# Mixer of a streaming conv encoder: branch a's output tiles ahead of its last six gate tiles, which become three block pairs

## The chip, the cores and the metric

The kernel runs on one core of one Trainium2 chip. The metric is the device time of one launch in microseconds (us). TensorE (PE in the profile) multiplies, VectorE (DVE) adds and multiplies elementwise, ScalarE (ACT) does activations, casts and scaled copies, GpSimd (POOL) here issues accumulating transfers and small copies, and SyncE (SP) issues the loads of the weights. Each engine works through its instructions in program order.

## The reference, cut to what matters

```python
x = x + 0.5 * swiglu_ffn(rms_norm(x, ffn1_norm), ...)          # first FFN
h = rms_norm(x, mix_norm);  p = h @ w_in                        # 1024 -> 7 * 1024
a_b, a_c, a_v, b_u, gate_a, gate_b = split(p)
y_a = (a_b * causal_depthwise_conv3(a_c * a_v)) @ w_a_out
glu = b_u[..., :D] * sigmoid(b_u[..., D:])
b_conv = causal_depthwise_conv31(glu)
b_act = silu(layer_norm(b_conv + bias, ln_g, ln_b))
y_b = b_act @ w_b_out
x = x + (sigmoid(gate_a) * y_a + sigmoid(gate_b) * y_b) @ w_out
x = x + 0.5 * swiglu_ffn(rms_norm(x, ffn2_norm), ...)           # second FFN, then a final norm
```

There are 512 prompt rows and 64 sample rows, T = 576 together; D is 1024 and everything is fp32.

## The kernel before

Features lie on the 128 partitions and the 576 rows of x along them, so a 1024-feature activation is eight tiles of 128x576 (KT = 8, KU = 4). A product of one output tile is a sum over the eight input tiles. To keep fp32 accuracy every operand is split into a high part (cast to fp32r, by ScalarE) and a low part (what the cast lost), and three matmuls (high x high, high x low, low x high) are made for each of two halves of 288 columns. A **plain tile** is therefore 8 x 3 x 2 = 48 matmuls of 128x288. For a pair of output tiles there is a second form, the **block pair**: a 2x2 block product with seven multiplications instead of eight (Winograd's form of Strassen's algorithm), where the two output tiles and the two column halves are the blocks. It takes seven blocks of 4 x 3 = 12 matmuls, each with weights of its own (four of the seven are sums of the loaded ones) and moving operands of its own (some are sums of the input's halves, made by `Forms`). VectorE combines the seven results q[0] to q[6] into the two tiles. The two FFNs are made of block pairs for the most part; in the mixer before the change only two pairs of branch b's output (`block_pair`) are.

**Weight units.** `Stream` takes the weights through in units of four k-chunks (128x512). A unit's load goes over SP's queue into one of six raw tiles. Then `begin` casts the high part (ScalarE), and for a unit planned with "dma" ScalarE writes the negative of the high part and GpSimd adds the raw weights onto it by an accumulating transfer; for a unit planned with "dve", `end` lets VectorE subtract. `add` makes the sums of a block pair (VectorE). `get(n)` comes just ahead of the matmuls of unit n and calls `lead`, which ends the units up to n+5, adds up to n+7 and begins up to n+6 (`ahead` is 6 here). The parts go to tiles "u" (pool of four, one per unit) or to two tiles of another pool ("act", 44 of 128x576). A raw tile is loaded anew when its last reader is through.

**Order of work.** The order is the program's, on each engine. `product` issues the matmuls of a tile, then runs the evacuation (`then`) of the product before it (`take`), then `fill` takes steps out of the list `work` as long as a planned VectorE clock lags the planned TensorE clock. PSUM has four tiles of two banks (`psum2`); a block takes one bank.

**The mixer.** Eight tile pairs of p3/p4 (branch b's value and gate), whose 31-tap convolution is in `work`, then for branch a the tiles of p1, p2, p0. In the stretch that the change is about the kernel does, for j = 0 to 7, `product(("p", 5, j))` (gate a; `ga_of` takes the sigmoid) and `product(("ya", j))` (`ya_of` multiplies by the gate into M[j], which is the tile of X[j]). Between them `advance()` carries the LayerNorm of branch b through its stages: gather the sum, multiply it by ones on TensorE (`total`), the mean `mu`, eight `center` steps (subtract, square on ScalarE, add), gather the squares, and `rstd` (again a product with ones, then a root on ScalarE and three VectorE steps) for RL. After that come eight gate b tiles `product(("p", 6, j))` with the steps of `swish` in `work`, then yb (plain, block, plain, block pair) and the product with w_out.

The two lines of the loop that set the order, and the plan's homes of gate b's units:

```python
product(("p", 5, j), xg, ga_of(j))
advance()
product(("ya", j), AB, ya_of(j))
advance()
few = cycle(("u", "u", "u", "act"))
```

Of the kernel before, what the change touches and what calls it, by code (L numbers as in the profile page):

```python
# [9 lines left out]
F32 = mybir.dt.float32  # L10
F32R = mybir.dt.float32r
I32 = mybir.dt.int32
AF = mybir.ActivationFunctionType
ALU = mybir.AluOpType

P = 128
D = 1024
KT = D // P
# [4 lines left out]
KU = KT // 2  # L23
T = SEQ + DSEQ
# [89 lines left out]
def tile_encoder_step(  # L114
# [7 lines left out]
    pe, dve, sca, pool = (  # L122
        Ordered(tc, e, c)
        for e, c in (
            (nc.tensor, pe_cost), (nc.vector, dve_cost), (nc.scalar, None), (nc.gpsimd, None)
        )
    )
# [13 lines left out]
    def nm(s):  # L141
        uid[0] += 1
        return f"{s}_{uid[0]}"
# [4 lines left out]
    def gtile(dt=F32, n=LB, at=0):  # L148
        return conv.tile([P, 640], dt, tag="g", name=nm("g"))[:, at : at + n]
# [10 lines left out]
    def wtile(dt=F32, n=LB - HB):  # L160
        return conv.tile([P, LB - HB], dt, tag="w", name=nm("w"), bufs=6)[:, :n]

    def ttile(dt=F32):
        return tmp.tile([P, T], dt, tag="tmp", name=nm("tmp"))
# [13 lines left out]
    def halves(ap):  # L178
        return ap.rearrange("p (s n) -> p s n", s=2)

    def half(ap, s):
        return ap[:, s * H : (s + 1) * H]
# [148 lines left out]
    def home(other):  # L331

        homes[0] += 1
        return ("u", other)[homes[0] % 2]
# [24 lines left out]
    def plan_block(name, raws, homes, lows=("dma", "dma", "dma")):  # L359

        a21, a22, a11, a12 = raws
        s1, s2, s3, s4 = ((name, n) for n in range(1, 5))
        plan[name] = [
            ws.unit(src, KU, home, how, sums)
            for home, (src, how, sums) in zip(homes, (
                (a11, lows[0], ((s1, (a21, a22)),)),
                (s2, "dve", ((s2, (s1, a11)),)),
                (s1, "dve", ()),
                (s3, "dve", ((s3, (a11, a21)),)),
                (a12, lows[1], ()),  # L370
                (s4, "dve", ((s4, (s2, a12)),)),
                (a22, lows[2], ()),
            ))
        ]
        for n, unit in enumerate(plan[name]):
            second = n in (1, 5, 6)
            ws.places[unit] = (SHIFT, 0) if second else (0, SHIFT)
# [26 lines left out]
    def plan_mixer(name, w, col, home_of=None, low="dma"):  # L404
        plan_tile(name, w, 0, (KU, KU), col, "act", home_of, low)
# [4 lines left out]
    for j in range(KT):  # L410
        for b in (1, 2, 0):
            plan_mixer(("p", b, j), w_in, b * D + j * P)
    for j in range(KT):
        plan_mixer(("p", 5, j), w_in, 5 * D + j * P)
        plan_mixer(("ya", j), w_a_out, j * P)

    few = cycle(("u", "u", "u", "act"))
    for j in range(KT):
        plan_mixer(("p", 6, j), w_in, 6 * D + j * P, few)


# [44 lines left out]
    def block(w, xs):  # L466

        q = bank()[:, :H]
        for k in range(KU):
            (whi, wlo), (xh, xl) = w, xs[k]  # L470
            for m, (l, r) in enumerate(((whi, xh), (whi, xl), (wlo, xh))):
                pe.matmul(q, l[:, k, :], r, start=k == m == 0, stop=k == KU - 1 and m == 2)
        return q
# [10 lines left out]
    def take():  # L484

        while behind:
            ready, then = behind.pop(0)
            dve.time = max(dve.time, ready)
            then()
# [11 lines left out]
    def product(name, xs, then=None, order=None, got=None, soon=None):  # L501


        if name in early:
            return early.pop(name)[:, :, :H]
        ps = psum2()
        if order:
            got = chunks(name)
            for n, k in enumerate(order):
                mm(ps, *got[k], xs[k], n == 0, n == len(xs) - 1)  # L510
        else:
            turn, turning[0] = turning[0], False
            k = 0
            for n in plan[name]:
                w = None
                if not got:
                    w = ws.get(n)
                end = k + ws.units[n][1]
                k0 = k
                while k < end:  # L520
                    w = got[k][0] if got else w
                    if turn and k == 0:
                        turned(ps, w, xs)
                        k += 2
                        continue
                    mm(ps, w, k - k0, xs[k], k == 0, k == len(xs) - 1)
                    k += 1
                    if soon and k == 1:
                        soon()
        take()  # L530
        if then is None:
            dve.time = max(dve.time, pe.time)
            return ps[:, :, :H]
        fill()
        behind.append((pe.time, lambda: then(ps[:, :, :H])))
# [15 lines left out]
    def high(v):  # L551
        hi = atile(F32R)
        sca.copy(hi, v)
        return hi

    def low(v, hi):
        lo = atile(F32R)
        dve.tensor_tensor(lo, v, hi.bitcast(F32), op=ALU.subtract)
        return lo
# [115 lines left out]
    class Forms:  # L675
# [21 lines left out]

        def split(self, p):
            self.parts[p] = [(hi, low(v, hi)) for v, hi in self.t.pop(p)]

        def operands(self, xg):

# [444 lines left out]
    def center(j, mu):  # L1147

        dve.tensor_tensor(C[j], C[j], mu, op=ALU.subtract)
        var.square(C[j])  # L1150
        var.add(dve)

    def swish(i, RL, sig={}):

        if i < KT:
            dve.tensor_tensor(C[i], C[i], RL, op=ALU.mult)
            sig[i] = ttile()
            sca.activation(sig[i], C[i], AF.Sigmoid, scale=par(i, R_LG), bias=par(i, R_LB))
        j = i - 1
        if 0 <= j < KT:  # L1160
            dve.tensor_scalar(
                C[j], C[j], par(j, R_LG), par(j, R_LB), op0=ALU.mult, op1=ALU.add
            )
            dve.tensor_tensor(sig[j], sig[j], C[j], op=ALU.mult)
            BA.append(high(sig[j]))
        j = i - 2
        if 0 <= j < KT:
            BA[j] = (BA[j], low(sig[j], BA[j]))
            forms.b.setdefault(j // 2, []).append(sig[j])

    def ga_of(j):
        def then(ps):
            t = gates[j] = ttile()
            sca.activation(halves(t), ps, AF.Sigmoid)
        return then

    def ya_of(j):
        def then(ps):
            dve.tensor_tensor(halves(M[j]), ps, halves(gates.pop(j)), op=ALU.mult)
        return then  # L1180

    stage, held = [0], [0]

    def advance():

        nonlocal var, mu, RL
        if stage[0] == 0 and len(C) == KT and not work:
            lnsum.gather()
        elif stage[0] == 1:
            mu = ttile()  # L1190
            sca.mul(halves(mu), lnsum.total(), 1.0 / D)
            turning[0] = True
            var = Sum()
            work.extend((lambda i=i: center(i, mu)) for i in range(KT))
        elif stage[0] == 2 and not work:
            var.gather()
        elif stage[0] == 3 and not held[0]:
            held[0] = 1
            return
        elif stage[0] == 3:  # L1200
            RL = rstd(var)
            turning[0] = True
        else:
            return
        stage[0] += 1

    var = mu = RL = None
    for j in range(KT):
        if j == 5:
            while len(C) < KT:  # L1210
                work.pop(0)()
        product(("p", 5, j), xg, ga_of(j))
        advance()
        product(("ya", j), AB, ya_of(j))
        advance()
    take()
    sca.dma_start(hist.rearrange("(j p) n -> p j n", p=P), hst)
    while stage[0] < 4:
        while work:
            work.pop(0)()  # L1220
        advance()
    for i in range(KT + 2):
        work.append(lambda i=i: swish(i, RL))

        if i in (3, 5):
            work.append(lambda p=(i - 3) // 2: forms.combine(p))
        if i in (4, 6):
            work.append(lambda p=(i - 4) // 2: forms.split(p))
    ws.ahead = 4

    def gb_of(j):
        def then(ps):
            while work and j >= 2 and len(BA) < j - 1:
                work.pop(0)()
            sg = wtile(n=T) if j < 2 else gtile(n=T)
            sca.activation(halves(sg), ps, AF.Sigmoid)
            SGB.append(sg)
        return then

    for j in range(KT):  # L1240
        product(("p", 6, j), xg, gb_of(j))
    while work:
        work.pop(0)()
    for p in range(KU // 2, KU):
        forms.combine(p)
    take()
    for p in range(KU // 2, KU):
        forms.split(p)
# [227 lines left out]
```

## Time and profile before

| | |
|---|---|
| median of 3 runs | 1287.54 us (1287.22 to 1287.66) |
| profiled execution, its own time | 1287.41 us |
| its span | 1285.6 us |
| busy: TensorE, VectorE, ScalarE, GpSimd | 1275.0, 927.8, 762.8, 357.2 us |
| matmuls | 9728 |
| mean granted TensorE clock | 0.998 |

The span is the time from the first to the last instruction of the profiled execution; 1.8 us of its own time lie outside. All positions in the text are microseconds from the start of that span. In the stretch in question gate a and ya run from about 643.4 to 744.4, gate b to 794.3, yb after it. In a row of the timeline the first number is the start, the second the length, then engine, line, operation, written tile <- read tiles, form and count; the bracket gives the idle time of the engine ahead of it and what ended that. All rows have line 90, since one helper issues every instruction.

### The profile page before, as it was taken

The page shows a single profiled execution, that of the slowest core. Times are in us where ns is not written, and L with a number is a line of the kernel's source. Part 1 is how long each engine was busy: PE and PEld are TensorE (multiplying, and loading weights), DVE is VectorE, ACT ScalarE, POOL GpSimd, SP SyncE. Part 2 cuts the span into 40 slices and gives each one's busy share as a digit, 9 for nine tenths or more (in the row PEclk, how much of TensorE's full clock was granted, in tenths as well). Part 3 has the DMA queues.
Part 4 walks back from the last instruction along what each step waited for, and adds up shares of the span by engine and source line. Part 5 has one row for each costly group of instructions (what it writes and reads, how often), then busy time and mean ns, then how long its engine had stood idle before and what let it go on. Part 6 is the DMA issues. An engine that isn't in the chain of part 4 may idle for free.

```text
span 1285.6 us, 25688 instructions
## 1 busy us (share of the span) xinstructions
PE 1275.0 (99%) x9728; PEld 1273.3 (99%) x9728; DVE 927.8 (72%) x1544; ACT 762.8 (59%) x1354; POOL 357.2 (28%) x455
## 2 busy tenths in 40 slices
PE   9999999999999999999999999999999999999997
PEld 9999999999999999999999999999999999999996
DVE  6868668748846998888895166756967848847955
ACT  7645646646776645555444576467665655654664
POOL 0032332332333444333321221122142141241230
PEclk9999999999999999999999999999999999999999
DMA  7287786886799898878885767686597696796693
GB/s 222 69 181 154 164 181 154 178 183 147 157 225 230 173 207 166 172 168 177 169 169 124 170 137 160 147 207 147 132 177 174 147 203 147 165 207 140 153 181 93
DMA packets 286091, 213.94 MB, mean 166 GB/s; under 512 B 15376, under 2 KB 248848, under 8 KB 285968
## 3 DMA queue, kind: packets, MB, share of 16 engines
q0 software_dynamic: 55440, 91.12, 43.3%
q1 hardware_dynamic: 228784, 120.35, 32.9%
q8 instruction: 77, 1.26, 0.4%
q10 hardware_dynamic: 1744, 0.83, 0.2%
q14 instruction: 46, 0.38, 0.1%
HBM read 116.17 MB, written 4.98 MB: 94 GB/s over the span
## 4 chain that ended last, share of the span: by engine, by line
PE 98%; DMA 1%; DVE 0%; ACT 0%; SPq 0%; DVEq 0%; issue 0%
PE mm L90 98%; DMA x<-in_x_dram 0%; DMA gains<-in_params_dram 0%; DVE g L90 0%; DVE tmp L90 0%; SPq L730 0%; DVE act L90 0%; ACT act L90 0%; DVEq L1466 0%; DVE r L90 0%; DVE x L90 0%; ACT tmp L90 0%; ACT r L90 0%
## 5 line engine op out<-in xcount | busy, mean ns | idle before, releaser
L90 PE MATMUL mm<-act,u 128*128 128x288 f32 x4758 | 666.2, 293 | 0.0
L90 PEld LDWEIGHTS mm<-act,u 128*128 128x128 f32 x4758 | 637.2, 188 | 0.0
L90 PE MATMUL mm<-act,g 128*128 128x288 f32 x3030 | 431.5, 293 | 0.0
L90 PEld LDWEIGHTS mm<-act,g 128*128 128x128 f32 x3030 | 408.9, 188 | 0.3 <-DMA g<-raw 0.2
L90 POOL DMA_DIRECT2D u<-raw x194 | 169.3, 873 | 477.1 <-ACT u L90 311.6
L90 PE MATMUL mm<-act,act 128*128 128x288 f32 (+2 forms) x1896 | 258.8, 293 | 0.5 <-DVE act L90 0.3
L90 PEld LDWEIGHTS mm<-act,act 128*128 128x128 f32 x1896 | 251.1, 188 | 1.1 <-DVE act L90 0.6
L90 ACT CAST u<-raw 128x512 fp32r<-128x512 f32 (+2 forms) x207 | 118.9, 575 | 172.3 <-PE mm L90 142.0
L90 POOL DMA_DIRECT2D g<-raw x124 | 107.8, 869 | 302.5 <-ACT g L90 246.4
L90 DVE SCALAR_TENSOR_TENSOR w<-g,prm,w 128x606 f32<-128x606 f32 x232 | 179.3, 842 | 1.4 <-ACT w L90 1.4
L90 DVE TENSOR_TENSOR tmp<-mm,tmp 128x288 f32<-128x288 f32 (+1 forms) x251 | 112.7, 457 | 67.3 <-PE mm L90 50.9
L90 ACT ACTIVATE u<-u 128x512 fp32r<-128x512 f32 (+2 forms) x194 | 115.0, 593 | 6.2
L90 ACT CAST g<-raw 128x512 fp32r<-128x512 f32 (+2 forms) x136 | 75.1, 552 | 45.6 <-DMA raw<-in_ffn_w_down_dram 16.3
L90 DVE SCALAR_TENSOR_TENSOR tmp<-mm,r 128x576 f32<-128x576 f32 x48 | 36.3, 756 | 74.8 <-PE mm L90 74.8
L90 POOL DMA_DIRECT2D act<-raw x67 | 59.1, 883 | 107.9 <-ACT act L90 94.2
L90 ACT CAST act<-tmp 128x576 fp32r<-128x576 f32 x92 | 61.9, 675 | 43.6 <-DVE tmp L90 42.5
L90 ACT CAST g<-w 128x512 fp32r<-128x512 f32 x79 | 49.0, 620 | 63.4 <-DVE w L90 55.8
L90 ACT CAST u<-w 128x512 fp32r<-128x512 f32 x81 | 50.2, 619 | 59.5 <-DVE w L90 43.3
L90 DVE TENSOR_TENSOR act<-tmp,act 128x576 fp32r<-128x576 f32 x92 | 67.5, 754 | 18.4 <-ACT act L90 16.8
L90 ACT ACTIVATE g<-g 128x512 fp32r<-128x512 f32 (+2 forms) x124 | 70.9, 572 | 3.9
L90 DVE TENSOR_TENSOR w<-raw,raw 128x512 f32<-128x512 f32 x82 | 56.1, 684 | 16.6 <-DMA raw<-in_ffn_w_gate_up_dram 12.1
L90 ACT ACTIVATE tmp<-tmp 128x576 f32<-128x576 f32 x47 | 32.2, 685 | 44.1 <-DVE tmp L90 44.1
(86 smaller groups left out, 833.4 us busy)
## 6 DMA issues: line engine op xcount, KB each, us to landing
raw<-in_ffn_w_gate_up_dram SPq DMA_DIRECT2D x171, 256.0 KB, 3.4
u<-raw POOLq DMA_DIRECT2D x137, 256.0 KB, 4.1
raw<-in_w_in_dram SPq DMA_DIRECT2D x112, 256.0 KB, 3.9
raw<-in_ffn_w_down_dram SPq DMA_DIRECT2D x96, 192.0 KB, 3.8
g<-raw POOLq DMA_DIRECT2D x67, 256.0 KB, 4.0
act<-raw POOLq DMA_DIRECT2D x61, 256.0 KB, 4.3
g<-raw POOLq DMA_DIRECT2D x43, 192.0 KB, 4.5
u<-raw POOLq DMA_DIRECT2D x41, 192.0 KB, 4.5
```

The source lines that it names most:

```text
L90: return self.tc.keep_in_program_order(fn(*args, **kwargs))
```

## The change

Gate a's tiles 0 and 1 stay plain and come first. Then come the eight ya tiles: the first two are multiplied by their gates as before, the other six are copied to M[j] by ScalarE. The six other gate a tiles are made after that by three block pairs (`gate_pair`), and each result goes through the sigmoid and is multiplied onto M[j]. The block pairs need sums of the input's halves: `whole` adds each input tile's high and low part on VectorE and combines them (two calls with tiles of pool "w", two with "act" tiles, behind ya3 to ya6), and `part` splits the results (four calls ahead of gate b's tile 0, four ahead of tile 1). Gate b's tiles 0 and 1 lie between ya and the block pairs, tiles 2 to 7 behind them. `center` adds the square of the step before ahead of making its own. `mu` gets a tile of another pool. Of `swish`, steps 0 and 1 come ahead of the block pairs, the others go with `work` from gate b's tile 2 on, in a new order with `parted`, and in C[j] instead of a second tile; the tiles of gate b from 2 on wait in the program's order for the combining that frees their room.

```diff
-    for j in range(KT):
+    for j in range(2):
         plan_mixer(("p", 5, j), w_in, 5 * D + j * P)
+    for j in range(KT):
         plan_mixer(("ya", j), w_a_out, j * P)
     few = cycle(("u", "u", "u", "act"))
-    for j in range(KT):
+    for j in range(2):
+        plan_mixer(("p", 6, j), w_in, 6 * D + j * P, few)
+    for i in range(1, KU):
+        plan_block(("p5", "s", i), [
+            ws.raw(w_in, h * KU * P, KU, 5 * D + j * P)
+            for j in (2 * i + 1, 2 * i) for h in range(2)
+        ], [home("act") for _ in range(7)])
+    for j in range(2, KT):
         plan_mixer(("p", 6, j), w_in, 6 * D + j * P, few)
...
+        def whole(self, p, xs, make):
+            b1, b2 = d, _ = [make(n=T) for _ in range(2)]
+            for b, (hi, lo) in zip((b1, b2), (xs[p], xs[p + KU])):
+                dve.tensor_tensor(b, hi.bitcast(F32), lo.bitcast(F32), op=ALU.add)
+            c = ttile()
+            ...  # the four half-width steps of combine
+            self.t[p] = [c, d]
+        def part(self, p):
+            v = self.t[p].pop(0)
+            hi = high(v)
+            self.parts.setdefault(p, []).append((hi, low(v, hi)))
...
     def center(j, mu):
         dve.tensor_tensor(C[j], C[j], mu, op=ALU.subtract)
+        var.add(dve)
         var.square(C[j])
-        var.add(dve)
...
     def ya_of(j):
         def then(ps):
-            dve.tensor_tensor(halves(M[j]), ps, halves(gates.pop(j)), op=ALU.mult)
+            if j in gates:
+                dve.tensor_tensor(halves(M[j]), ps, halves(gates.pop(j)), op=ALU.mult)
+            else:
+                sca.copy(halves(M[j]), ps)
...
-            mu = ttile()
+            mu = rpool.tile([P, T], F32, tag="r", name=nm("mu"), bufs=2)
...
+    xforms = Forms()
+    for j in range(2):
+        product(("p", 5, j), xg, ga_of(j))
     for j in range(KT):
-        if j == 5:
+        if j == 3:
             while len(C) < KT:
                 work.pop(0)()
-        product(("p", 5, j), xg, ga_of(j))
-        advance()
         product(("ya", j), AB, ya_of(j))
+        if j in (3, 4):
+            xforms.whole(j - 3, xg, wtile)
+        if j in (5, 6):
+            xforms.whole(j - 3, xg, atile)
         advance()
     take()
     sca.dma_start(hist.rearrange("(j p) n -> p j n", p=P), hst)
-    while stage[0] < 4:
+    while stage[0] < 3:
         while work:
             work.pop(0)()
         advance()
+    for p in range(KU):
+        xforms.part(p)
+    product(("p", 6, 0), xg, gb_of(0))
+    while stage[0] < 4:
+        advance()
+    for p in range(KU):
+        xforms.part(p)
+    product(("p", 6, 1), xg, gb_of(1))
+    swish(0, RL)
+    swish(1, RL)
+    bs = xforms.operands(xg)
+    later = []
+    def gate_pair(i):
+        ...  # steps as in block_pair
+        def first():
+            dve.tensor_tensor(half(c1, 1), q[5], u4, op=ALU.add)
+            sca.activation(c1, c1, AF.Sigmoid)
+        def last():
+            dve.tensor_tensor(half(c2, 0), q[6], u3, op=ALU.add)
+            sca.activation(c2, c2, AF.Sigmoid)
+        def gated(j, t):
+            dve.tensor_tensor(M[j], M[j], t, op=ALU.mult)
+        for n, xs in enumerate(bs):
+            q.append(block(ws.get(plan["p5", "s", i][n]), xs))
+            if n > 0:
+                steps[n - 1]()
+            take()
+            if later:
+                later.pop(0)()
+        later.extend((last, lambda: gated(j, c1), lambda: gated(j + 1, c2)))
+    for i in range(1, KU):
+        gate_pair(i)
...
-    for j in range(KT):
+    for j in range(2, KT):
         product(("p", 6, j), xg, gb_of(j))
```

More of the change, by code (lines that the diff above doesn't have):

```diff
@@ L412, in tile_encoder_step @@
             plan_mixer(("p", b, j), w_in, b * D + j * P)
+    for j in range(2):
+        plan_mixer(("p", 5, j), w_in, 5 * D + j * P)
     for j in range(KT):
-        plan_mixer(("p", 5, j), w_in, 5 * D + j * P)
         plan_mixer(("ya", j), w_a_out, j * P)
     few = cycle(("u", "u", "u", "act"))
-    for j in range(KT):
+    for j in range(2):
[6 more added lines that the diff above has]
+    for j in range(2, KT):
         plan_mixer(("p", 6, j), w_in, 6 * D + j * P, few)
@@ L699, in split @@
             self.parts[p] = [(hi, low(v, hi)) for v, hi in self.t.pop(p)]
+        def whole(self, p, xs, make):
[3 more added lines that the diff above has]
+            c = ttile()
+            for out, a, b, op in (
+                (half(c, 0), half(b1, 0), half(b1, 1), ALU.subtract),
+                (half(c, 1), half(b2, 1), half(c, 0), ALU.add),
+                (half(d, 0), half(b1, 1), half(b2, 1), ALU.subtract),
+                (half(d, 1), half(b2, 0), half(c, 1), ALU.subtract),
+            ):
+                dve.tensor_tensor(out, a, b, op=op)
+            self.t[p] = [c, d]
[3 more added lines that the diff above has]
+            self.parts.setdefault(p, []).append((hi, low(v, hi)))
         def operands(self, xg):
@@ L1163, in swish, with parted @@
             )
-            dve.tensor_tensor(sig[j], sig[j], C[j], op=ALU.mult)
-            BA.append(high(sig[j]))
-        j = i - 2
+            dve.tensor_tensor(C[j], sig.pop(j), C[j], op=ALU.mult)
+    def parted(i):
+        if i < KT:
+            BA.append(high(C[i]))
+        j = i - 1
         if 0 <= j < KT:
-            BA[j] = (BA[j], low(sig[j], BA[j]))
-            forms.b.setdefault(j // 2, []).append(sig[j])
+            BA[j] = (BA[j], low(C[j], BA[j]))
+            forms.b.setdefault(j // 2, []).append(C[j])
     def ga_of(j):
@@ L1178, in then, with gb_of, combined @@
         def then(ps):
-            dve.tensor_tensor(halves(M[j]), ps, halves(gates.pop(j)), op=ALU.mult)
-        return then
+            if j in gates:
+                dve.tensor_tensor(halves(M[j]), ps, halves(gates.pop(j)), op=ALU.mult)
+            else:
+                sca.copy(halves(M[j]), ps)
+        return then
+    def gb_of(j):
+        def then(ps):
+            while work and j >= 2 and joined[0] <= (j - 2) // 2:
+                work.pop(0)()
+            sg = wtile(n=T) if j < 2 else gtile(n=T)
+            sca.activation(halves(sg), ps, AF.Sigmoid)
+            SGB.append(sg)
+        return then
+    joined = [0]
+    def combined(p):
+        forms.combine(p)
+        joined[0] += 1
     stage, held = [0], [0]
@@ L1221, in tile_encoder_step, with second @@
         advance()
-    for i in range(KT + 2):
+    for p in range(KU):
[11 more added lines that the diff above has]
+    def gate_pair(i):
+        j = 2 * i
+        c1, c2, qu, uu = (ttile() for _ in range(4))
+        q1, u2, u3, u4 = half(qu, 0), half(qu, 1), half(uu, 0), half(uu, 1)
+        q = []
+        def second():
+            dve.tensor_tensor(u3, q[3], u2, op=ALU.add)
+            dve.tensor_tensor(half(c2, 1), u3, q[2], op=ALU.subtract)
+        def first():
[6 more added lines that the diff above has]
+            dve.tensor_tensor(M[j], M[j], t, op=ALU.mult)
+        steps = (
+            lambda: sca.copy(q1, q[0]),
+            lambda: dve.tensor_tensor(u2, q[1], q1, op=ALU.subtract),
+            lambda: dve.tensor_tensor(u4, q[2], u2, op=ALU.subtract),
+            second,
+            lambda: dve.tensor_tensor(half(c1, 0), q[4], q1, op=ALU.add),
+            first,
+        )
+        for n, xs in enumerate(bs):
[6 more added lines that the diff above has]
+        later.extend((last, lambda: gated(j, c1), lambda: gated(j + 1, c2)))
@@ L1223, in tile_encoder_step @@
+    for i in range(1, KU):
+        gate_pair(i)
+    while later:
+        later.pop(0)()
+    spare.clear()
+    for i in range(2, KT + 1):
         work.append(lambda i=i: swish(i, RL))
-        if i in (3, 5):
-            work.append(lambda p=(i - 3) // 2: forms.combine(p))
+        if i > 1:
+            work.append(lambda i=i: parted(i - 2))
         if i in (4, 6):
-            work.append(lambda p=(i - 4) // 2: forms.split(p))
-    ws.ahead = 4
[L1231 to L1238, printed above, removed]
@@ L1240, in tile_encoder_step @@
-    for j in range(KT):
+            work.append(lambda p=(i - 4) // 2: combined(p))
+        if i in (5, 7):
+            work.append(lambda p=(i - 5) // 2: forms.split(p))
+    for i in range(KT - 1, KT + 1):
+        work.append(lambda i=i: parted(i))
+    ws.ahead = 4
+    for j in range(2, KT):
         product(("p", 6, j), xg, gb_of(j))
@@ L1244, in tile_encoder_step @@
     for p in range(KU // 2, KU):
-        forms.combine(p)
+        combined(p)
     take()
```

## The prediction

> **What bounds the kernel now.** I read the page first (engines, slices, chain), then the timeline of the mixer engine by engine, then the transfers.
>
> ```profile
> span 1285.6 us, 25688 instructions
> ...
> PE 1275.0 (99%) x9728; PEld 1273.3 (99%) x9728; DVE 927.8 (72%) x1544; ACT 762.8 (59%) x1354; POOL 357.2 (28%) x455
> ...
> PEclk9999999999999999999999999999999999999999
> ...
> PE 98%; DMA 1%; DVE 0%; ACT 0%; SPq 0%; DVEq 0%; issue 0%
> ```
>
> TensorE is busy for 99% of the span, the chain that ended last is TensorE for 98%, and the granted clock is full in all 40 slices. No other engine is near. So a matmul taken out is time gained, and any wait put into TensorE's order is time lost: the whole question is whether the new operands are there when TensorE comes to them. The profiled execution (1287.41 us) is 0.13 us under the median of the runs (1287.54), so a sum made on it needs no correction.
>
> The timeline of TensorE in the mixer:
>
> ```profile
> 687.09 0.69 PE L90 MATMUL mm<-tmp,ones_r 128*128 128x288 f32 x4
> ...
> 712.61 0.69 PE L90 MATMUL mm<-tmp,ones_r 128*128 128x288 f32 x4
> ...
> 738.13 3.28 PE L90 MATMUL mm<-act,act 128*128 128x288 f32 x24
> ...
> 794.29 3.28 PE L90 MATMUL mm<-act,u 128*128 128x288 f32 x24
> ...
> 806.77 1.74 PE L90 MATMUL mm<-act,u 128*128 128x288 f32 x12
> ...
> 817.82 3.31 PE L90 MATMUL mm<-act,u 128*128 128x288 f32 x24
> ```
>
> The row at 794.29 opens yb's tiles 0 and 1, 806.77 is the first block of yb's block pair, 817.82 the next plain tile. Two plain tiles take 12.48 us (6.24 each, 130 ns a matmul); a block pair takes 11.05 (1.58 a block). The rows with four matmuls from `ones_r` are LayerNorm's two products with ones: mean at 687.09, variance at 712.61, 0.53 each. A change in the time of less than 0.2%, 2.6 us, I count as no change.
>
> **Gain.** Three pairs at 12.48 - 11.05 = 1.43: **-4.3 us**. The other products keep their matmuls. Up to the first block pair TensorE has as much to do as before, only in another order: p5_0, p5_1, ya0 to ya4, mean's product at 687.1, ya5 to 693.9, ya6 to 700.1, ya7 to 706.3, gate b's tile 0 to 712.6, variance's product to 713.1, gate b's tile 1 to **719.35**. There the first pair begins; call its weight units B0 to B6, due at 719.35 + 1.58 n.
>
> **How early a block's weights have to be begun.** Units are begun six ahead of their use: in plain tiles 6 x 3.12 = 18.7 us, in blocks 6 x 1.58 = 9.5. An FFN block pair shows what is kept in steady state (TensorE, ScalarE, VectorE):
>
> ```profile
> 302.06 1.75 PE L90 MATMUL mm<-act,g 128*128 128x288 f32 x12
> ...
> 311.53 1.75 PE L90 MATMUL mm<-act,g 128*128 128x288 f32 x12
> ```
>
> ```profile
> 301.34 0.61 ACT L90 CAST u<-raw 128x512 fp32r<-128x512 f32 x1
> ```
>
> ```profile
> 311.73 0.46 DVE L90 TENSOR_TENSOR tmp<-mm,tmp 128x288 f32<-128x288 f32 x1 [0.52 <-PE mm L90]
> ```
>
> VectorE's row adds q[5] and waits for TensorE, whose next block starts at 311.53; q[5] is the sixth block, so B0 started six blocks earlier, at 302.06, and ScalarE began its B6 at 301.34, 0.7 us earlier. What a "dma" unit then takes, from these rows (GpSimd; transfers):
>
> ```profile
> 657.66 0.86 POOL L90 DMA_DIRECT2D u<-raw  x1 [3.67 <-ACT u L90]
> ```
>
> ```profile
> u<-raw POOLq DMA_DIRECT2D x137, 256.0 KB, 4.1
> raw<-in_w_in_dram SPq DMA_DIRECT2D x112, 256.0 KB, 3.9
> ```
>
> Cast and negative take 1.2 us on ScalarE (below, 656.73 is such a negative, ending at 657.36, and GpSimd issues 0.3 later), the accumulation lands 4.1 after its issue: 5.6 in all. B6 is due 9.5 + 0.3 after B0 (the low part is its third matmul), so ScalarE may reach B6's cast at most 4.2 us after B0's start. A second limit is tighter: the raw tile of B6 is the one that the next pair's a12 is loaded into. 5.6 + load 3.9 + 5.6 = 15.1 later a12's low part is there, due 11 blocks + 0.3 = 17.7 after B0. Hence the **cover is 2.6 us**. What ScalarE and VectorE have ahead of that cast is costed now.
>
> **ScalarE and VectorE in the stretch before** (ScalarE, then VectorE):
>
> ```profile
> 656.73 0.63 ACT L90 ACTIVATE u<-u 128x512 fp32r<-128x512 f32 x1
> ...
> 687.82 0.65 ACT L90 ACTIVATE tmp<-mm 128x576 f32<-128x576 f32 x1 [5.36 <-PE mm L90]
> ...
> 691.25 0.67 ACT L90 ACTIVATE acc<-g 128x576 f32<-128x576 f32 x1
> 691.82 0.67 ACT L90 ACTIVATE tmp<-g 128x576 f32<-128x576 f32 x1
> ...
> 713.08 1.28 ACT L90 ACT_TABLE_LOAD   x1
> 714.37 0.65 ACT L90 ACTIVATE r<-mm 128x576 f32<-128x576 f32 x1
> ...
> 738.33 0.62 ACT L90 CAST u<-raw 128x512 fp32r<-128x512 f32 x1 [4.42 <-PE mm L90]
> ...
> 747.69 0.62 ACT L90 CAST u<-raw 128x512 fp32r<-128x512 f32 x1 [1.83 <-PE mm L90]
> ...
> 748.88 0.63 ACT L90 ACTIVATE tmp<-mm 128x576 f32<-128x576 f32 x1
> ...
> 759.50 1.81 ACT L90 CAST act<-tmp 128x576 fp32r<-128x576 f32 x3
> ```
>
> ```profile
> 678.64 0.76 DVE L90 TENSOR_TENSOR acc<-acc,g 128x576 f32<-128x576 f32 x1
> 680.14 0.76 DVE L90 TENSOR_TENSOR tmp<-acc,tmp 128x576 fp32r<-128x576 f32 x1 [0.74 <-ACT tmp L90]
> ...
> 688.50 1.43 DVE L90 TENSOR_TENSOR g<-g,tmp 128x576 f32<-128x576 f32 x2 [6.70 <-ACT tmp L90]
> 692.53 0.76 DVE L90 SCALAR_TENSOR_TENSOR acc<-acc,tmp 128x576 f32<-128x576 f32 x1 [2.60 <-ACT tmp L90]
> 693.21 0.75 DVE L90 TENSOR_TENSOR g<-g,tmp 128x576 f32<-128x576 f32 x1
> ...
> 715.06 0.76 DVE L90 SCALAR_TENSOR_TENSOR tmp<-r 128x576 f32<-128x576 f32 x1 [3.55 <-ACT r L90]
> ...
> 716.71 0.76 DVE L90 SCALAR_TENSOR_TENSOR r<-tmp,r 128x576 f32<-128x576 f32 x1
> ...
> 758.45 0.45 DVE L90 TENSOR_TENSOR tmp<-tmp 128x288 f32<-128x288 f32 x1
> 758.93 1.20 DVE L90 TENSOR_TENSOR tmp<-tmp,tmp 128x288 f32<-128x288 f32 x3
> 760.05 0.75 DVE L90 TENSOR_TENSOR g<-g,r 128x576 f32<-128x576 f32 x1
> ...
> 796.17 0.68 DVE L90 TENSOR_TENSOR w<-w,raw 128x512 f32<-128x512 f32 x1
> 796.77 0.68 DVE L90 TENSOR_TENSOR w<-raw,raw 128x512 f32<-128x512 f32 x1
> ```
>
> Look at 738.33. The cast into a "u" tile is one that the program puts six units ahead, in front of the first unit of the tile p5_7, and yet it ran when that tile had ended on TensorE (738.13): gate b's first three units all go to "u", and four "u" tiles are soon used up. Behind it everything on ScalarE is late: 748.88 is the sigmoid of p5_7, 10.7 us after its product. Before the change this costs nothing, since LayerNorm is through by 717.5 and nothing waits. After it, gate b's tiles 0 and 1 come right behind ya, and the same three casts (u, u, u) come in front of ya5's two units and ya6's first.
>
> *To the mean: no cost.* The taps end where they did: the same taps stand in front of the row 678.64, VectorE is busy with them throughout, and their number and lengths don't change. `whole` is two adds at 0.67 and four half steps (758.45 to 760.05, 1.6): 2.9. One, then the gather (2.26, from 678.64 to 680.90), then another: 686.8, the gather being over at 683.9 for the product at 687.1. Centring starts at 688.50 as before.
>
> *Squares: 4.6 us late.* The cast for gate b's unit 1 waits for ya5's "u" tile: 693.9 + 0.2. Cast, negative (1.2) and ya4's copy (0.57, the step from 691.25 to 691.82) bring ScalarE to 695.9 for the first square (691.25 before), and VectorE's first add to 697.1 instead of 692.53.
>
> *VectorE to the variance: 713.3.* From 697.1: seven more adds and subtractions at 0.67 to 701.8, `whole` to 704.7, first weight sum (0.60, row 796.17 to 796.77) to 705.3, four steps to 708.0, `whole` to 711.0, gather to 713.3. The late add of the square saves its waits (692.53 to 694.71 for a step that now takes 1.35), but two `whole` of 2.9 stand in the chain. The product is due at 712.6: **stall 0.7**.
>
> *PSUM: stall 1.2.* ScalarE casts B1 behind VectorE's second sum (713.9), and behind that stand ya6's and ya7's copies, to 715.0 and 715.5. Gate b's tile 1 needs ya6's PSUM tile and starts at 715.1, not 713.9. B0 moves to 721.4.
>
> *Parts and root.* Four casts at 0.57 (759.50: three in 1.81) to 717.8, their four low parts to 718.9, B1's low part, third sum and B2's low part to 720.8; B3's cast to 720.9; table load 1.28 and root 0.65 (713.08, 714.37) to 722.9; three VectorE steps 2.41 (715.06 to 717.47) to 725.3. Four more casts to 725.1, B4 to 726.3 (landed 730.7); four low parts to 728.0, B3's low part to **728.7**, fourth sum to 729.2. B5's cast 729.9, table back 731.2, gate b's sigmoid **731.8**, two of `swish` 733.2; B5's low part **734.0**; **B6 begun 733.2**, landed **739.0**.
>
> *TensorE.* B3, at 726.1, waits for its low part: 2.4. B4 has no PSUM until the sigmoid at 731.8 frees gate b's tile 0: 1.8. B5: 0.3. B6 waits for the accumulation: 3.4. With 0.7 and 1.2 this is 9.8 for the first pair. Second pair: a12 at 739.0 + 3.9 + 5.6 = 748.5, due 740.4 + 6.6 = 747.0: 1.5. Third pair the same way, its B6 being begun on time for the most part: 0.7. **Stalls 12.0.** The same from the cover: 733.2 - 719.35 = 13.9 late, less 2.6, is 11.3; I take 12.
>
> *What costs nothing, and its cover.* Within a pair VectorE has 4 sums, 4 low parts, 7 half steps, 2 multiplications, 9 us; ScalarE 7 casts, 3 negatives, copy, 2 sigmoids, 8 us, both under 11.05. Loads stay 32 for gate a and gate b, on SP's queue in another order (gate b's first two tiles ahead of the pairs); accumulations on GpSimd's queue fall by 3 (3 of 7 units a pair instead of all 4). The copies of ya take the place of multiplications off the path. `swish` has six tiles, 37.4 us, in front of yb; without that cover a late BA would stall yb, bounded by 0 and by the two steps' 3 us that I take as 0. `mu`'s other tile: nothing, two tiles of that pool being enough.
>
> **Sum:** 1287.4 - 4.3 + 12.0 = **1295.1 us**.
>
> The row 714.37 follows the table load's end at once. [...]
>
> **The rivals.**
>
> 1. *All is hidden, faster: 1283.1.* Speaks for it: FFN pairs run without a gap. Against: there B6 is begun 0.7 us ahead of B0. It decides at a delay of 1.7 us, that is, B6 begun by 723.7. But even with ScalarE and VectorE free at the variance's product the root ends at 715.0, RL at 717.5, low parts, B3's and the fourth sum at 721.4, B5's cast at 722.0, table and three sigmoids at 725.4: 6.0 late, 3.4 over the cover, 1286.5. Only shorter transfers could make it faster.
> 2. *Half of it: 1286.5 to 1291.* The "u" wait doesn't bite the squares, or is made good: the chain is 4.6 us earlier, B6 begun at 728.6, 6.7 over the cover, 1289.8. For it: the lag at 748.88 had built up over several tiles. Against: the wait needs only one.
> [...]
> 4. *Stalls later too:* yb waits for BA by the 3 us bound above, 1298. Against: VectorE idles between some of these rows even now.
>
> **How the numbers follow.** The sum's own case, 1291 to 1297.5: 0.52. Rival 1: 0.08. Rival 2: 0.24 (0.20 of it within 2.6 us, that is under 1290.1). Rival 3: 0.10. Rival 4: 0.06. Faster 0.08, same 0.20, slower 0.72. The range leaves out rival 1 and the far ends of 3 and 4: 1286.4 to 1300.5; my likeliest case alone, 1291 to 1297.5.
>
> **What the profile after would show.** Right: TensorE idle between 712 and 760, the longest gap ahead of the last block of the first pair and put down to a transfer on GpSimd's queue; gaps in front of B3 (VectorE) and B4 (ScalarE); the first square near 696, right behind a cast that waited for TensorE; the variance's product late; pairs two and three nearly without gaps. Wrong: TensorE without a gap and 4.3 us less span (rival 1), the first square near 691 (rival 2), slices with a lower granted clock (3), gaps in front of yb (4). Most likely to fail is the place of some step in the program's order, since the whole chain hangs together: each 1 us that it is shorter takes 1 us off the time.

## The result: slower by 1.7%

| | before | after |
|---|---|---|
| median | 1287.38 us (1286.21 to 1287.66, 4 runs) | 1309.36 us (1308.64 to 1311.25, 4 runs) |
| span of the profiled execution | 1285.6 us | 1307.5 us |
| matmuls | 9728 | 9692 |
| TensorE: start of yb in the profile | 794.29 | 815.11 |

The ratio is 1.0173, with an interval of 1.0157 to 1.0189: 22 us more, where 7.7 more was forecast. The page of the changed kernel, engines, clock and chain:

```profile
span 1307.5 us, 25740 instructions
...
PE 1278.9 (98%) x9692; PEld 1275.6 (98%) x9692; DVE 967.9 (74%) x1621; ACT 773.9 (59%) x1377; POOL 354.0 (27%) x452
...
PEclk9999999999999999999999898999999999999998
...
PE 88%; issue 6%; DVE 2%; DMA 1%; ACT 1%; POOL 0%; DVEq 0%; POOLq 0%; ACTq 0%
```

TensorE is still the bound, but now 12% of the chain that ended last isn't TensorE. Its busy time even rose by 3.9 us with 36 matmuls fewer, and three of the 40 slices have a lower granted clock: the 23rd and the 25th, counted from 1, both in the mixer, and the last, before whose end TensorE has finished its work. TensorE's list of waits (us in total, times, longest) names what it waited for; these are its first six rows (before, the longest wait of TensorE was 1.0):

```profile
PE mm L90 <- ACT u L90: 6.7, 1, 6.7
PE mm L90 <- DMA u<-raw: 3.3, 2, 3.0
PE mm L90 <- DMA act<-raw: 2.2, 1, 2.2
PE mm L90 <- DVE u L90: 1.9, 1, 1.9
PE mm L90 <- ACT w L90: 1.6, 1, 1.6
PE mm L90 <- ACT x L90: 1.2, 1, 1.2
```

The timeline of TensorE in the mixer places them:

```profile
713.30 0.66 PE L90 MATMUL mm<-tmp,ones_r 128*128 128x288 f32 x3 [0.39 <-DVE tmp L90]
715.13 3.42 PE L90 MATMUL mm<-act,u 128*128 128x288 f32 x24 [1.17 <-ACT x L90]
...
728.63 1.57 PE L90 MATMUL mm<-act,u 128*128 128x288 f32 x10 [1.90 <-DVE u L90]
731.83 3.25 PE L90 MATMUL mm<-act,act 128*128 128x288 f32 x12 [1.63 <-ACT w L90]
734.88 2.76 PE L90 MATMUL mm<-act,u 128*128 128x288 f32 x12
737.48 0.43 PE L90 MATMUL mm<-act,act 128*128 128x288 f32 x2
740.10 2.42 PE L90 MATMUL mm<-act,act 128*128 128x288 f32 x10 [2.20 <-DMA act<-raw]
742.32 2.49 PE L90 MATMUL mm<-act,u 128*128 128x288 f32 x12
744.65 1.74 PE L90 MATMUL mm<-act,act 128*128 128x288 f32 x12
...
765.17 9.64 PE L90 MATMUL mm<-act,u 128*128 128x288 f32 x72
...
791.02 1.33 PE L90 MATMUL mm<-act,u 128*128 128x288 f32 x4 [6.73 <-ACT u L90]
795.31 4.36 PE L90 MATMUL mm<-act,u 128*128 128x288 f32 x20 [2.96 <-DMA u<-raw]
...
815.11 3.28 PE L90 MATMUL mm<-act,u 128*128 128x288 f32 x24
```

There are two stretches of loss.

*The first pair* (713 to 745). The pairs would have ended at 719.35 + 3 x 11.05 = 752.5 without a stall; they end at 765.17, **12.7 late**. The five waits are 7.3 of it (0.39 + 1.17 + 1.90 + 1.63 + 2.20). The slower matmuls between them are 4.1: the blocks at 731.83, 734.88 and 742.32 take 3.05, 2.60 and 2.33 us to the next row instead of 1.58, and the ten matmuls at 740.10 take 2.22 instead of 1.32. Most of the last 1.3 is the end of the row before each wait: a row that nothing follows at once is 0.17 to 0.27 longer than its matmuls at 130 ns.

*Gate b's tiles 2 to 7* (765.17 to 815.11). They take 49.94 us where six plain tiles take 37.44: **12.5 late**. Two waits are 9.7 of it, 6.73 for ScalarE's cast and 2.96 for the accumulation behind it, and the slow matmuls right after them nearly all the rest, 2.8 (granted clock 0.50 from 791.02 to 792.35, 0.63 from 795.31 to 799.67).

So -4.3 + 12.7 + 12.5 = 20.9, the shift of yb's start (815.11 - 794.29 = 20.8). The last 1.1 us are lost at the very end: VectorE's last row of outputs ends at 1281.66 before and at 1302.46 after, 20.8 apart, but the span goes on for 3.9 us behind it before and for 5.0 after, until the output transfers have landed. Why they land later stays open.

The windows of the profile (us, busy time and count of TensorE, its weight loads, VectorE, ScalarE and GpSimd, granted clock, DMA share, GB/s) for the first pair, for gate b's last six tiles, and for one narrow stretch:

```profile
721.50:742.40 20.90, 15.17 (x87) 14.45 (x86) 16.53 (x28) 15.67 (x26) 3.47 (x4) 0.79 0.40 87
...
765.20:815.10 49.90, 40.21 (x289) 39.62 (x289) 32.38 (x57) 28.82 (x47) 6.88 (x8) 0.90 0.58 130
```

```profile
731.80:735.20 3.40, 3.37 (x14) 3.37 (x15) 2.56 (x5) 3.37 (x6) 0.00 (x0) 0.50 0.14 41
```

TensorE has work for all of 731.8 to 735.2 and gets through 14 matmuls in 3.4 us, since the granted clock is 0.50.

What held up the first pair is in the timelines of ScalarE and VectorE:

```profile
693.89 0.62 ACT L90 CAST u<-raw 128x512 fp32r<-128x512 f32 x1 [4.45 <-PE mm L90]
...
695.60 0.69 ACT L90 ACTIVATE acc<-g 128x576 f32<-128x576 f32 x1
...
720.91 1.28 ACT L90 ACT_TABLE_LOAD   x1
722.21 0.65 ACT L90 ACTIVATE r<-mm 128x576 f32<-128x576 f32 x1
...
731.13 0.65 ACT L90 ACTIVATE w<-mm 128x576 f32<-128x576 f32 x1
...
733.19 0.61 ACT L90 CAST act<-raw 128x512 fp32r<-128x512 f32 x1
733.84 0.63 ACT L90 ACTIVATE act<-act 128x512 fp32r<-128x512 f32 x1
...
736.08 0.38 ACT L90 COPY tmp<-mm 128x288 f32<-128x288 f32 x1
```

```profile
696.90 0.76 DVE L90 SCALAR_TENSOR_TENSOR acc<-acc,tmp 128x576 f32<-128x576 f32 x1 [6.49 <-ACT tmp L90]
...
712.48 0.76 DVE L90 TENSOR_TENSOR tmp<-acc,tmp 128x576 fp32r<-128x576 f32 x1 [0.74 <-ACT tmp L90]
...
727.89 0.68 DVE L90 TENSOR_TENSOR u<-w,u 128x512 fp32r<-128x512 f32 x1
```

The cast at 693.89 waits for TensorE to give up a "u" tile, and the first square follows at 695.60; B3's low part ends at 728.57 and TensorE takes B3 at 728.63; gate b's sigmoid ends at 731.78 and TensorE goes on at 731.83. And of the second stretch, ScalarE and then GpSimd:

```profile
769.18 0.63 ACT L90 ACTIVATE u<-u 128x512 fp32r<-128x512 f32 x1
...
772.55 0.87 ACT L90 ACTIVATE tmp<-g,prm 128x576 f32<-128x576 f32 x1 [1.59 <-DVE g L90]
...
789.59 0.87 ACT L90 ACTIVATE tmp<-g,prm 128x576 f32<-128x576 f32 x1
790.36 0.60 ACT L90 CAST u<-raw 128x512 fp32r<-128x512 f32 x1
```

```profile
736.72 0.86 POOL L90 DMA_DIRECT2D act<-raw  x1 [9.25 <-ACT tmp L90]
...
791.92 0.86 POOL L90 DMA_DIRECT2D u<-raw  x1 [20.95 <-ACT u L90]
```

Between 769.18 and 790.36 ScalarE begins no weight unit at all. It does two sigmoids of the last pair and then the activations and casts of `swish`, one tile after another, most of them waiting for VectorE; all six of its sigmoids that are left (772.55 the first, 789.59 the last) stand ahead of the next weight cast; GpSimd meanwhile has no accumulation for 20.95 us. TensorE runs out of weights in the middle of that.

### The profile page after: what moved, and what is told of

The parts are those of the page before. It is cut to its first block, busy times and chain, and to the rows that moved or that the text cites. A ratio compares the mean times of both kernels' runs of the same rounds, so it can differ in the third digit from the quotient of the medians.

```text
span 1307.5 us, 25740 instructions
## 1 busy us (share of the span) xinstructions
PE 1278.9 (98%) x9692; PEld 1275.6 (98%) x9692; DVE 967.9 (74%) x1621; ACT 773.9 (59%) x1377; POOL 354.0 (27%) x452
## 4 chain that ended last, share of the span: by engine, by line
PE 88%; issue 6%; DVE 2%; DMA 1%; ACT 1%; POOL 0%; DVEq 0%; POOLq 0%; ACTq 0%
PE mm L90 88%; DVE tmp L90 1%; DMA u<-raw 1%; DVE act L90 0%; DVE acc L90 0%; DVE g L90 0%; DVE w L90 0%; DMA act<-raw 0%; DMA gains<-in_params_dram 0%; ACT tmp L90 0%; DMA raw<-in_ffn_w_gate_up_dram 0%; ACT act L90 0%; ACT g L90 0%; ACT u L90 0%; ACT w L90 0%
## 5 line engine op out<-in xcount | busy, mean ns | idle before, releaser
L90 DVE TENSOR_TENSOR tmp<-mm,tmp 128x288 f32<-128x288 f32 (+1 forms) x269 | 120.8, 458 | 74.8 <-PE mm L90 55.4
L90 POOL DMA_DIRECT2D g<-raw x120 | 104.6, 872 | 254.2 <-ACT g L90 187.4
L90 ACT CAST u<-w 128x512 fp32r<-128x512 f32 x86 | 53.2, 619 | 70.4 <-DVE w L90 53.1
L90 ACT CAST act<-tmp 128x576 fp32r<-128x576 f32 x88 | 58.8, 676 | 43.5 <-DVE tmp L90 42.5
L90 DVE TENSOR_TENSOR act<-tmp,act 128x576 fp32r<-128x576 f32 x88 | 64.5, 754 | 19.3 <-ACT act L90 17.7
L90 DVE TENSOR_TENSOR w<-raw,raw 128x512 f32<-128x512 f32 x88 | 60.3, 685 | 16.7 <-DMA raw<-in_ffn_w_gate_up_dram 12.6
L90 DVE TENSOR_TENSOR w<-w,raw 128x512 f32<-128x512 f32 x88 | 60.2, 684 | 2.6 <-DMA raw<-in_ffn_w_gate_up_dram 1.8
```

Of the source, the lines that this page charges most:

```text
L90: return self.tc.keep_in_program_order(fn(*args, **kwargs))
```

## The experiments

All ratios below are against the kernel before, which ran beside each group of experiments: its median was 1287.38 us beside the change, 1286.76 in experiments 1 to 4, 1287.15 in 5 to 8 and 1287.07 in 9. A difference in us between the change and an experiment is therefore uncertain by about 0.6. The theory after the result: the second stretch comes from the planner. `fill` in `product` is

```python
while work and dve.time < pe.time - AHEAD:
    work.pop(0)()
```

and `product` raises VectorE's planned clock to TensorE's in `take`, when there is a product to evacuate, or at its end; `gate_pair` calls `take` too, but once gate b's tile 1 is evacuated in its first block there is nothing left that would raise the clock. After three block pairs VectorE's planned clock is then far behind, so the first product of gate b empties most of `work` into the program at once, ahead of the casts of later weight units, which then stand behind it in ScalarE's order. The rival was that gate b's tiles wait for the room that the combining frees.

**1. VectorE's planned clock raised behind the pairs.**

```diff
+    dve.time = max(dve.time, pe.time)
     ws.ahead = 4
     for j in range(2, KT):
```

> The changed kernel, with one line added behind the last block pair: the planned VectorE clock is set to the planned TensorE clock if it lags. Theory P (planner): block pairs don't move that clock on, so it lags behind them, the first plain tile's fill pops nearly all swish steps at once, and the weight casts of gate b's later tiles stand behind them on ScalarE (no cast from 769.2 to 790.4). Then the second stretch of waits, 12.5 us between 765 and 815, is gone: 1297 us (1296 to 1299), and the first stretch (B0 to the end of the third pair) stays as it is. Theory R (room): the tiles of gate b from 2 on wait for room that the combining frees, and the order in which their evacuation pops steps holds up the casts whatever the clock says: 1306 to 1310.

Measured: 1296.60 us (1294.98 to 1300.71), ratio 1.0085 (1.0066 to 1.0105). Its window over gate b's last tiles, and TensorE's row for B6:

```profile
765.20:815.10 49.90, 49.90 (x382) 49.90 (x381) 40.76 (x69) 34.36 (x57) 7.74 (x9) 1.00 0.68 156
```

```profile
740.18 1.59 PE L90 MATMUL mm<-act,act 128*128 128x288 f32 x10 [3.05 <-DMA act<-raw]
```

TensorE is busy for 49.90 of 49.90 us and the clock is full, where it was 40.21 and 0.90; gate b's last six tiles take 37.9 us (763.72 to 801.64) instead of 49.94. One line of the planner's bookkeeping is worth 12.8 us by the medians, 12.0 of it in these tiles. Since the line does nothing unless the planned clock lags, this shows the theory of the planner; that of the room falls, since the homes and the order of the combining are as they were. The first pair still has its waits, the one at B6 3.05 instead of 2.20. In the profiled execution the pairs also end 1.4 earlier than in the change (763.72 and 765.17), which the edit can't have done, standing behind them: the instructions up to there are the same, but fewer of the matmuls are slow: the block at 734.88 takes 1.83 us to the next row instead of 2.60, the ten behind B6's wait 1.44 instead of 2.22, and the block behind those 1.58 instead of 2.33.

**2. Gate b's tiles 0 and 1 not in "u" three times of four.**

```diff
     for j in range(2):
-        plan_mixer(("p", 6, j), w_in, 6 * D + j * P, few)
+        plan_mixer(("p", 6, j), w_in, 6 * D + j * P)
```

> The changed kernel, with the four weight units of gate b's tiles 0 and 1 planned in turn to act and u tiles, like those of ya, instead of u, u, u, act. Theory U (the cast that waits for a u tile holds up the squares): the first square moves from 695.6 to about 691.2, the chain to the last weight unit of the first pair is 4 to 4.6 us earlier, and so are its waits: 1305 us (1303.5 to 1306.5). Rival (the chain is bound elsewhere, by whole's and the centring's VectorE steps or by ScalarE's other work): 1308 to 1310.

Measured: 1303.92 us (1303.21 to 1305.01), 1.0132 (1.0117 to 1.0148), 5.4 us less than the change. The first square on ScalarE starts at 690.12, where it was 695.60. TensorE's timeline in the first pair:

```profile
726.30 1.86 PE L90 MATMUL mm<-act,act 128*128 128x288 f32 x12 [1.54 <-ACT w L90]
...
734.58 2.36 PE L90 MATMUL mm<-act,act 128*128 128x288 f32 x10 [3.66 <-DMA act<-raw]
```

The square is 5.5 earlier (0.9 of that is there already at the mean, 686.69 and not 687.62), it no longer stands behind a cast that waits for TensorE, and the waits at the variance's product and for PSUM are gone, so it was the cast into "u" that held up the squares. The waits at the sigmoid (1.54) and B6 (3.66) stay, and the second stretch is as in the change (waits of 6.72 and 2.96).

**3. The root moved behind the first pair, `swish` 0 and 1 behind the last.**

```diff
-    while stage[0] < 4:
-        advance()
     for p in range(KU):
         xforms.part(p)
...
-    swish(0, RL)
-    swish(1, RL)
...
     for i in range(1, KU):
         gate_pair(i)
+        while i == 1 and stage[0] < 4:
+            advance()
     while later:
         later.pop(0)()
+    swish(0, RL)
+    swish(1, RL)
```

> The changed kernel, with the root of the variance (its product with ones, table load, root, VectorE steps) behind the first block pair and swish's steps 0 and 1 behind the last pair; the splits of the sums stay ahead of gate b's tile 1. Theory T (the root's chain and the two table loads stand in front of the casts of B4, B5 and B6): the last unit of the first pair is begun some 8 to 10 us earlier, the first stretch loses 3 to 5 us instead of 12.9, the second stretch stays or grows by the two steps (0 to 3 us): 1300 us (1298 to 1304). Rival (the pair's own sums and low parts, or the raw tiles, are too slow in any case): 1306 to 1310.

Measured: 1302.73 us (1301.58 to 1306.61), 1.0128 (1.0109 to 1.0146), 6.6 less than the change. B6 is reached sooner, but still late:

```profile
729.31 1.59 PE L90 MATMUL mm<-act,act 128*128 128x288 f32 x10 [2.62 <-DMA act<-raw]
```

The pairs end at 758.67, with the variance's product now among them, 6.2 late where I had expected 3 to 5. The root with its two table loads and `swish`'s first steps, which were moved together, is thus a part of the delay of about the size of the "u" tiles, and not all of it. The second stretch stays (5.95 and 2.96).

**4. All three.**

> All three edits together (planned clock, homes, root behind the first pair). If theories P, U and T hold, TensorE waits little: the 4.3 us of matmuls saved remain, less 0 to 3 us of rest: 1283 to 1287 us against 1287.4 of before. If the pairs are too early in any case (raw tiles, sums), 1290 or more.

Measured: 1290.07 us (1287.66 to 1293.94, 9 runs), 1.0025 (1.0014 to 1.0036). This missed: I had expected the kernel to be at least as fast as before. The three edits make 19.3 us together and 24.8 added up. Experiment 5 shows 1 and 2 to be nearly additive, so the overlap is with 3, most likely because 2 and 3 shorten the same chain; 2 and 3 without 1 were not run. The profiled execution (1292.59 us) is 2.5 slower than the median. TensorE's list of waits shows what is left in it, beside two at the kernel's ends that were there before, all of it accumulations on GpSimd's queue:

```profile
PE mm L90 <- DMA act<-raw: 4.6, 3, 2.2
PE mm L90 <- DMA u<-raw: 1.7, 2, 1.3
```

The largest is in yb's block pair, and the matmuls behind it are slow too (ten in 2.74 us instead of 1.59; the granted clock from 818.40 to 821.80 is 0.65):

```profile
819.36 2.74 PE L90 MATMUL mm<-act,act 128*128 128x288 f32 x10 [2.23 <-DMA act<-raw]
```

**5. Edits 1 and 2 only.** Do the two stretches add?

> The changed kernel with two edits, the planned clock set behind the pairs and gate b's first tiles in act and u tiles in turn. If the two stretches of waits have separate causes, the gains add: 12.5 and 5.5 us off 1309.4, 1291.5 us (1290 to 1293.5). If clearing the one moves waits into the other, less: 1294 to 1297.

Measured: 1292.25 us (1291.54 to 1295.76, 10 runs), 1.0037 (1.0026 to 1.0048). 17.1 us of the 18.2 that they bring alone: nearly additive, as expected, since they lie in different stretches.

**6. The squares as they were before.** The one part of the change that isn't needed for the block pairs, undone:

```diff
     def center(j, mu):
         dve.tensor_tensor(C[j], C[j], mu, op=ALU.subtract)
-        var.add(dve)
         var.square(C[j])
+        var.add(dve)
```

> The changed kernel with the old order in center: the square of a step is added in the same step, so VectorE waits for ScalarE in every step. If VectorE's chain from the squares to the last unit of the first pair sets the first stretch, six waits of 0.7 us come back: 1313 us (1311.5 to 1315), the waits lying in front of the variance's product and the first pair. If the late squares bought nothing because ScalarE was behind in any case: 1308 to 1310.5.

Measured: 1313.71 us (1312.67 to 1314.90), 1.0198 (1.0179 to 1.0218), 4.4 more than the change. The variance's product now waits 6.68 us:

```profile
718.38 0.61 PE L90 MATMUL mm<-tmp,ones_r 128*128 128x288 f32 x1 [6.68 <-ACT tmp L90]
```

So the square added a step later is worth 4.4 us. The chain from the squares to B6 is one chain: what this costs at the variance it takes off some later waits (the one at B3 is gone).

**7. Edits 1 to 3, and the last low part of the first two pairs made by VectorE** instead of an accumulation.

```diff
-        ], [home("act") for _ in range(7)])
+        ], [home("act") for _ in range(7)], ("dma", "dma", "dve" if i < 3 else "dma"))
```

> The kernel with all three edits (planned clock, homes, root behind the first pair), and besides the last weight unit of pairs one and two has its low part made by VectorE and not by the accumulating transfer. What is left of waits in front of these two blocks (0.4 and 1.9 us, both put down to that transfer) goes if the way of 5.6 us over GpSimd's queue is what makes it late: 1287 to 1288.5. If ScalarE's or VectorE's lag is the cause whatever way the low part takes, 1290 as with the three edits.

Measured: 1287.93 us (1286.30 to 1290.16, 10 runs), 1.0002 (0.9991 to 1.0013): no difference from before. The time is as forecast, but not all of the reason is. Of the two waits named, the one of 0.4 ahead of the first pair's last block is gone. The other, of 1.93 in experiment 4, I had put at the second pair's last block; by the count of TensorE's rows it stands at the third pair's first block, which this edit doesn't touch. It is still there, at 0.81. And yb's wait of 2.23 is down to 0.19 with no edit there. So part of the gain is not explained.

**8. As 7, with VectorE also making the last low part of yb's first block pair, the variance's gather behind the input's splits, and `swish` 0 and 1 behind the second pair.**

```diff
-        advance()
+        if j < 6:
+            advance()
...
-    while stage[0] < 3:
+    while stage[0] < 2:
...
+    while stage[0] < 3:  # behind the second four parts
+        advance()
...
+        if i == 2:  # behind gate_pair(i)
+            swish(0, RL)
+            swish(1, RL)
```

> As f3_lows, and besides: the variance's gather behind the splits (it is no longer needed before the first pair), swish's steps 0 and 1 behind the second pair instead of the third, and the last unit of yb's first block pair with VectorE's low part. If ScalarE's lag in front of the first pair, the swish steps late and the one accumulation in yb (2.2 us) are the rest, TensorE waits less than 1 us and the saved matmuls show: 1283.5 to 1285.5 against 1287. If the rest of the waits only moves, 1286 to 1289.

Measured: 1285.61 us (1284.97 to 1286.35, 12 runs), 0.9979 (0.9969 to 0.9990). This is the first version that is faster than before: its slowest run is below the fastest of the 29 of before (1286.44). The ratio makes it 2.7 us (1.3 to 4.0), but four of those 29 lie at 1290.8 to 1292.4; by the medians it is 1.5, by the spans of the two profiles 2.1. The time is just above the range that I expected, and TensorE's waits are more than the 1 us that I expected at most. yb starts at 792.36, 1.9 earlier than before, with two waits left in the mixer, 0.46 and this:

```profile
743.99 1.59 PE L90 MATMUL mm<-act,act 128*128 128x288 f32 x10 [2.22 <-DMA act<-raw]
```

1.9 + 0.46 + 2.22 is 4.6: the gain of three pairs (4.3) is there, less what TensorE still waits.

**9. As 8, with the first low part of the second and third pair made by VectorE too.**

```diff
-        ..., ("dma", "dma", "dve" if i < 3 else "dma"))
+        ..., ("dma" if i == 1 else "dve", "dma", "dve" if i < 3 else "dma"))
```

> As f4_more, and besides the first weight unit of the second and third pair has its low part made by VectorE. The two waits that f4_more has left in the pairs, 0.5 and 2.2 us, both put down to an accumulating transfer and both in front of a pair's first block, go if the way over GpSimd's queue is again what makes the unit late behind the root's two table loads: 2 to 2.7 us less than f4_more (1285.6), 1283 to 1283.7, and 0.28 to 0.33% faster than before, near the 4.3 us of the saved matmuls. If ScalarE's late cast alone holds these blocks up, 1284.5 to 1286.

Measured: 1285.43 us (1284.05 to 1286.20, 11 runs), 0.9984 (0.9975 to 0.9993). This missed by some 2 us: no different from 8. The time lies in the range of the other reading, a late cast on ScalarE, but that isn't shown by it, since the waits of 0.46 and 2.22 are both gone. Others have come:

```profile
751.66 1.59 PE L90 MATMUL mm<-act,act 128*128 128x288 f32 x10 [1.10 <-DMA act<-raw]
754.63 8.60 PE L90 MATMUL mm<-act,u 128*128 128x288 f32 x64 [0.32 <-DMA u<-raw]
```

yb starts at 791.15, still 1.2 earlier than in 8. Two more waits, of 0.96 and 0.39, are in the second FFN, in code that no edit touches, and they take that back. Why they come there stays open.

## Why the prediction was wrong in size

**The step that failed** is the one on what costs nothing: "`swish` has six tiles, 37.4 us, in front of yb". That cover is there and yb did not wait. But the steps of `swish` cost by where they stand, not by when they are due: the planner put them ahead of the casts for gate b's own tiles, and 12.5 us were lost between 765 and 815, where I had written 0. Rival 4 had a stall later on, but at yb and bounded by 3 us, which was wrong in place, mechanism and size. I had read `fill` as a rule that spreads the steps and didn't ask in what state the pairs leave the clock that it compares. Experiment 1 shows the cause. The forecast was 14.3 us too low: 12.5 from here, 0.7 from the first pair and 1.1 from the end of the kernel, which had no term in the sum.

**The term for the first pair** came out right in sum, 12.7 against 12.0, by two errors that cancel. Waits of TensorE were forecast at 12.0 and measured at 7.3; the slower clock was forecast at 0 in the sum and measured at 4.1, with 1.3 more around the waits. That the sum fits is luck. Step by step:

- Forecast and found: the first square at 695.9 (695.60), the first add at 697.1 (696.90), the variance's product stalled 0.7 (0.39), gate b's tile 1 at 715.1 (715.13), root's end 722.9 (722.86), B3's low part 728.7 (728.57), gate b's sigmoid 731.8 (731.78), B6 begun at 733.2 (733.19). Every one is within 0.4 us, so here a chain over four engines could be worked out from single rows.
- B3 and B4: 2.4 and 1.8 forecast, 1.90 and 1.63 measured; B5: 0.3 forecast, none measured.
- B6: landed at 739.0 by the forecast, TensorE went on at 740.10. Its negative ended at 734.47, but the accumulation was issued at 736.72, 2.25 later and not 0.3. The profile puts that down to ScalarE's copy of q[0] (736.08, ending at 736.46), and in experiments 1, 2 and 4 the accumulation also starts 0.26 behind the end of that copy. So it isn't chance; why the accumulation waits for a copy that it doesn't read stays open. The wait was still only 2.20 instead of 3.4, since TensorE itself came later by the slow blocks before it.
- Second and third pair: 1.5 and 0.7 forecast, none measured. From 742 to 765 TensorE has no wait in the change, most likely being late enough by then. In experiment 8, where it is earlier, the wait in the third pair is there (2.22).

**Rival 3**, to which I gave 0.10 as a case by itself, is that TensorE's granted clock falls after the waits. I had put it at 1.7 to 3.4 us, an assumption that no run shows. It happened as an addition: 4.1 us of slow matmuls in the first pair, and 2.8 more in gate b's tiles. The trace of the change has a granted clock of 1.00 in the ten matmuls right behind the wait of 1.90 us (728.63 to 730.20), and of 0.50 from 731.8 on, behind the next wait, of 1.63; the longest before these two was 1.17.

**The gain** of 4.3 us for three pairs was right: the third pair of the change, without a wait, takes 11.06 us (754.11 to 765.17), and experiment 8 accounts for 4.6. That the whole question is whether the operands are there was too narrow: PSUM's room (1.17 and 1.63) and the slow matmuls cost time as well. The cost of the two table loads by the row held as well: the root starts at 722.21, right behind 720.91 + 1.28, and gate b's sigmoid at 731.13, right behind the second load's 729.84 + 1.28.

## What to carry to other kernels

When part of a kernel that a planner interleaves by estimated clocks is rewritten, ask what each planned clock holds when the new part ends: a clock left behind turns "a little ahead" into "all at once", and the steps so issued stand in front of the next weights in each engine's order (here ScalarE began none from 769.18 to 790.36). When a bound engine at 99% is given a shorter form with twice as many weight units per matmul, the saving is the certain and small term; work out the chain that makes the first operands, and expect a wait to cost more than its own length where the clock falls behind it (7.3 us of waits came with 4.1 us of slow matmuls in the first pair). And a wait taken away from a chain with little slack can come back at its next weakest unit: three edits worth 24.8 us by themselves were worth 19.3 together, and the ninth run gained nothing.

## What of the hardware was not expected

The granted clock of TensorE falls after short waits, but not after each of them. In the change it is 0.50 after 1.90 and 1.63 within 5 us; in experiment 4 a single wait of 2.23 us is followed by ten matmuls in 2.74 us instead of 1.59; in experiment 8 a single one of 2.22 us is followed by ten in 1.59, at a granted clock of 1.00 (742.00 to 745.40). It differs even between the change and experiment 1, which have the same instructions up to there: ahead of B6 TensorE waits 2.20 in the one and 3.05 in the other, and the ten matmuls behind it take 2.42 us after the shorter wait, at a granted clock of 0.60 (740.10 to 742.32), and 1.59 after the longer. What decides it, these runs don't tell. Behind the longest one of experiment 5 ten matmuls took 1.52 us to the next row, near their usual 1.32, and only the block after them was slow (2.88 instead of 1.58; the granted clock from 735.20 to 738.60 is 0.69):

```profile
735.19 1.72 PE L90 MATMUL mm<-act,act 128*128 128x288 f32 x10 [3.66 <-DMA act<-raw]
736.71 3.08 PE L90 MATMUL mm<-act,u 128*128 128x288 f32 x12
739.59 1.90 PE L90 MATMUL mm<-act,act 128*128 128x288 f32 x12
```
